# A fifth block problem with seven products in the FFN, its first two products in the opening, and the rest rows inside the output product

## The chip, the cores and the metric

The kernel runs on one core of one Trainium2 chip. TensorE (PE; its weight loads are PEld) multiplies, VectorE (DVE) and ScalarE (ACT) work on elements, GpSimd (POOL) does a few small operations and issues the DMAs that add to their destination, and SyncE (SP) issues the other DMAs. The metric is the device time of one launch in microseconds (us); lower is better. A measured number is the median of several executions. Durations and waits come from one further execution that the hardware profiler recorded.

## The reference

Two layers over 512 rows of width 1024: a gated mixer of three branches (retention, chunked attention, differential attention), then a SwiGLU FFN, each followed by a normalisation. The change touches the FFN and its normalisation:

```python
D_MODEL, SEQ, DEPTH, FFN_HIDDEN = 1024, 512, 2, 2816
...
        x = _layer_norm(DEEPNORM_ALPHA * x + mix, ln1_g[l], ln1_b[l])

        u = jnp.einsum('bsd,df->bsf', x, w_ffn_in[l])
        u_gate, u_up = jnp.split(u, 2, axis=-1)
        ffn = jnp.einsum('bsf,fd->bsd', jax.nn.silu(u_gate) * u_up, w_ffn_out[l])
        x = _layer_norm(DEEPNORM_ALPHA * x + ffn, ln2_g[l], ln2_b[l])
```

All numbers are float32. The FFN's inner width 2816 is 22 tiles of 128.

## The kernel before

**Arithmetic.** Each float32 operand is carried as a pair of float32r tiles, the rounded part (`hi`) and what is left (`lo`). `mm3` (line 124) multiplies two pairs by three matmuls: hi by hi, hi by lo, lo by hi. A weight block (128 partitions x 2048, 1 MiB) is loaded into a staging buffer (`st`, four of them), cast by ScalarE to `wh` and subtracted by VectorE to `wl` (lines 157 and 158 in `Wt`, 315 and 322 in `Staged`). There are three `wh`/`wl` pairs (`AHEAD`). `run_items` works through a list of items; before an item runs it fetches the blocks of later ones until three are ready or in work. An item's `groups` are functions called at the `between()` places inside it. The tool that builds the program then orders the instructions of each engine by its own model of costs, with the program's order as priority, unless `keep_in_program_order` or `issue_after` ties them.

**Plain items.** `u_ffn(i)` makes one inner tile: `proj_T` for the gate and for the up part, each 8 steps of `mm3` with 512 moving columns, so 48 matmuls; the result stands transposed (features in partitions). ScalarE's silu and VectorE's product follow in `ffn_done`.

**Block problems.** `u_fin(pb, kind)` makes four inner tiles (512 gate and 512 up columns) at once. The product of two matrices of 2 x 2 blocks is made with seven block products in place of eight (m1, m2, y, x, v, g, h in `u_two`). Each product is one block of weights and `product(acts, name, j, wt)` for j = 0, 1: 4 steps of `mm3`, so 24 matmuls of 512 columns. The left operands are combinations of quarters of the input, made by `Quarters.left` (y, x) and `Quarters.right` (v, g); m1, m2 and h use quarters as they are, m1 and m2 those of the first 256 rows. The right operands are sums of weight blocks: made by DMA (`more`, a second DMA issued on POOL that adds to the staged block) or by VectorE (lines 254, 260 and 283). The class of the problem says which: `Chain` keeps one buffer from m1 to h and adds to it three times; `Close` and `Early` load a sum `a` (for y), a sum `c` (for g), and add `d` and `e` on VectorE; `Early` loads the block for `e` a second time in x. Products x, g and h add onto the PSUM banks of m1, and v onto those of y, so two banks are held from m1 to h and two from y to v. The results stand with rows in partitions; `s_turn` transposes them on TensorE (line 1444) and ScalarE copies them from PSUM.

Before, four block problems p, q, r, u make inner tiles 0 to 15, and `u_ffn(16)` to `u_ffn(21)` the six others. In the opening of the FFN, while the normalisation of the first half still goes on, stand p's m1, p's m2, `u_ffn(16)`, `u_ffn(17)`, `u_ffn(18)`, then p's y. The split of `u_ffn(16)`'s block is made in two parts (`half_split`, `s_other_half`). `s_turned(1)` makes the second 256 rows of the transposed input `x1T` (`to_T`: line 588, then `xTh` by ScalarE and `xTl` by VectorE); `s_x1` and `s_x1r` call `left` and `right`; `s_natural` scales and shifts the rows and stores them.

**Output product.** `fout_items(0)` and `(1)` (o and w) multiply inner tiles 0-3, 4-7 and 8-11, 12-15, again with seven products each. Their left operands are `Twins`, made by `s_ready`, `s_differ`, `s_sums` and `s_rest`. Inner tiles 16 to 21 (from `REST` on) go by plain products in `fout_rest`: for each of four row tiles t and two column halves, 6 steps of `mm3`, 18 matmuls. These stand at the very end, in `front`, `middle` and `back`; `plus` adds each result to `z` (lines 1298, 1300), the last one takes statistics (line 531), and `normalise` or, in the last layer, `finish` (lines 537 to 545) closes a row tile. In the last layer the very last tile is made in two halves of 256 columns. In layer 0, `transposes(0)` and `transposes(1)` stand midway in two tiles, `to_T(0)` follows, and `opening[l + 1].early()` loads the first block of the next layer; two more tiles stand behind them.

Of the kernel before, what the change touches and what calls it, by code (L numbers as in the profile page):

```python
# [58 lines left out]
def trunk(ctx, tc, x_in, xT_in, w_in, ret_norm_g, da_norm_g, lq1, lk1, lq2, lk2, w_a, w_b, w_c, b_merge, w_out,  # L59
# [26 lines left out]
    def bank(name="ps"):  # L86
        return psp.tile([P, 512], F32, tag="ps", name=name)
# [36 lines left out]
    def mm3(ps, lh, ll, rh, rl, start, stop, onto=False):  # L124
        nc.tensor.matmul(ps, lh, rh, start=start, stop=False, skip_group_check=onto)  # L125
        nc.tensor.matmul(ps, lh, rl, start=False, stop=False, skip_group_check=onto)  # L126
        nc.tensor.matmul(ps, ll, rh, start=False, stop=stop, skip_group_check=onto)  # L127
# [282 lines left out]
    def proj_T(act, wt, c0, nk=KT, ps=None, half=None):  # L410
# [281 lines left out]
    def layer(l):  # L692
# [714 lines left out]
        def ffn_spec(i):  # L1407
            w = w_ffn_in[l]
            return ([w[:, P * i:P * i + P], w[:, FFN + P * i:FFN + P * i + P]], KT)
# [95 lines left out]
        def half_split(i):  # L1505
            def fn():
                half_split.wt = w = Wt(*ffn_spec(i), later=True)
                w.load(0, KT)
                w.split(0, KT // 2)
                return w  # L1510
            return fn

        def s_other_half():
            half_split.wt.split(KT // 2, KT)

        def u_ffn(i):
            def fn(wt):
                pg = proj_T(x1T, wt, 0)
                between()
                pu = proj_T(x1T, wt, P)  # L1520
                ffn_done(i, pg, pu)
            return [half_split(i) if i == 16 else ffn_spec(i)], fn

        def fout_items(gi):

            r0, kh = GROUPS[gi]
            hv = Chain(w_ffn_out[l], r0, kh)
            w = {}

            def it(name, *adds):  # L1530
                def fn(wt):
                    if name == "m1" and gi == 0:
                        load_res(x2, saved[2 * l])
                    on = {"x": "m1", "g": "m1", "h": "m1", "v": "y"}.get(name, name)
                    for j in range(2):
                        w[on, j] = product([hid[r0 + k] for k in range(kh)], name, j, wt, w.pop((on, j), None))
                        for i, hf, op in adds:
                            plus(x2, 2 * i + j, hf, w[on, j], op)
                        if name in ("m2", "v", "h"):
                            w.pop((on, j))  # L1540
# [6 lines left out]
        def fout_rest():  # L1547

            A, B = slice(0, 256), slice(256, 512)
            rk = FT - REST - 4  # L1550
            b1, b3 = (([w_ffn_out[l][P * REST:P * REST + P * 4, 512 * hf:512 * hf + 512]], 4) for hf in range(2))
            b2 = ([w_ffn_out[l][P * REST + P * 4:P * FT, :]], rk)
            W, ahead = {}, {}

            def tile(t, hf, midway=None):
                at = [(W[("b1", "b3")[hf]], k, 0) for k in range(4)]
                at += [(W["b2"], k, 512 * hf) for k in range(rk)]
                end = last and t == NT - 1
                for cols in (A, B) if end and hf else (slice(0, 512),):
                    n = cols.stop - cols.start  # L1560
                    ps = bank("pf")[:, :n]
                    for i, (w, k, c) in enumerate(at):
                        if i == len(at) // 2 and midway:
                            midway()
                        a, sl, cs = hid[REST + i], slice(P * t, P * t + P), slice(c + cols.start, c + cols.stop)
                        mm3(ps, a.hi[:, sl], a.lo[:, sl], w.hi[:, k, cs], w.lo[:, k, cs], i == 0, i == len(at) - 1)
                    plus(x2, t, hf, ps, ALU.add, True, cols, (A, B) if end and not hf else (cols,))
                if hf:
                    x2["n"].finish(t) if last else x2["n"].normalise(t)

            def front(*_):
                x2["n"] = Norm(x2["z"], v["g2"], v["b2"], bcast_rows(ln2_g[l:l + 1]),
                               bcast_rows(ln2_b[l:l + 1]), xTs[l + 1], out if last else saved[2 * l + 1], xfs[l + 1])
                tile(0, 0)
                between()
                tile(1, 0)

            def middle(*_):
                if last:
                    for t, hf in (0, 1), (1, 1), (2, 0), (2, 1), (3, 0), (3, 1):  # L1580
                        tile(t, hf)
                    return
                n = x2["n"]
                tile(0, 1)
                opening[l + 1].early()
                tile(1, 1)
                tile(2, 0, lambda: n.transposes(0))
                tile(3, 0, lambda: n.transposes(1))
                n.to_T(0)
                ahead[nc.scalar] = last_of(nc.scalar)  # L1590

            def back(*_):
                tile(2, 1)
                tile(3, 1)
                quarters(l + 1)
                ahead[nc.vector] = last_of(nc.vector)
                behind[opening_fn[l + 1]] = list(ahead.values())

            def block(name, spec):

                def fn():
                    W[name] = Wt(*spec)
                    return W[name]
                return fn

            def held(name):
                return lambda: W[name]

            parts = [([block("b1", b1), block("b2", b2)], front), ([block("b3", b3), held("b1"), held("b2")], middle)]
            return [(p,) for p in parts + ([] if last else [([held("b2"), held("b3")], back)])]  # L1610

        p, q, r, u = u_fin(0, ffn_opening), u_fin(1, Close), u_fin(2, Close), u_fin(3, Close)
        proj["next"] = p["m1"][1]
        o, w = fout_items(0), fout_items(1)
        for (specs, fn), *groups in [
            (([ffn_opening.m1_high], p["m1"][1]), [], [s_turned(1)]), (([ffn_opening.m2_high], p["m2"][1]), [s_other_half], [s_natural(0)]), (u_ffn(16), [s_x1(0)], [s_x1(1)]),
            (u_ffn(17), [s_x1(2)], [s_x1(3)]), (u_ffn(18), [s_natural(1)], [s_x1r(0), p["c"]]), (p["y"], [s_x1r(1)], [s_x1r(2)]),
            (u_ffn(19), [s_x1r(3)], [s_natural(2)]), (p["v"], [s_natural(3)], [q["a"]]), (p["x"],), (q["m1"],), (p["g"],), (q["y"], [s_turn(0, 0)]), (p["h"], [q["c"]]),
            (q["v"], [r["a"]]), (q["m2"], [s_turn(0, 1)]), (q["x"],), (r["m1"],), (q["g"],), (r["y"], [s_turn(1, 0)]), (q["h"], [r["c"]]),
            (r["v"], [u["a"]]), (r["m2"], [s_turn(1, 1)]), (r["x"],), (u["m1"],), (r["g"],), (u["y"], [s_turn(2, 0)]),  # L1620
            (r["h"], [u["c"]], [s_ready(0, 0)]), (u["v"], [s_ready(0, 1)]), (u["m2"], [s_turn(2, 1)]), (u["x"],),
            (o["m1"], [s_differ(0, 0)], [s_differ(0, 1)]), (u["g"],), (o["m2"], [s_sums(0, 0)], [o["c"]]), (u["h"], [s_turn(3, 0)]),
            (o["y"], [s_sums(0, 1)]), (u_ffn(20), [s_rest(0, 0)], [s_rest(0, 1)]), (o["v"], [s_turn(3, 1)]),
            (o["x"], [s_ready(1, 0)], [s_ready(1, 1)]),
            (w["m1"], [s_differ(1, 0)]), (o["g"], [s_differ(1, 1)], [w["c"]]), (w["m2"], [s_sums(1, 0)]), (o["h"], [s_sums(1, 1)]),
            (w["y"], [s_rest(1, 0)]), (u_ffn(21), [s_rest(1, 1)], [s_hid(16, 17, 18)]), (w["v"], [s_hid(19, 20, 21)]), (w["x"],),
            (w["g"],), (w["h"],), *fout_rest(),
        ]:
            item(specs, fn, *groups)

# [59 lines left out]
```

## Time and profile before

| what | us |
|---|---|
| median of 3 runs | 1856.95 (1856.66 to 1857.39) |
| the profiled execution | 1857.49, its span 1855.7 |
| layer 0: opening of the FFN (p's m1) | from 588.6 |
| layer 0: first output product (o's m1) | from 781.8 |
| layer 1: opening of the FFN (p's m1) | from 1511.6 |
| layer 1: `u_ffn(16)` | from 1525.1 |
| layer 1: first output product (o's m1) | from 1704.8 |
| layer 1: rest rows | from 1815.4 |

Times inside are counted from the span's start. In a row of a group, "x" is the count, then come busy time, the mean length of one in ns, and the engine's idle time before them with what ended it. Matmuls overlap on TensorE: the length of one record is longer than the step from one to the next. In the view of the chain a row has start, share of the chain's time, and what.

### The profile page before, as it was taken

How to read it: one execution, taken by the hardware profiler on the slowest of the kernel's cores; microseconds unless marked ns; L12 is line 12 of the kernel's file. 1: busy time of each engine (PE TensorE's matmuls, PEld its weight loads, DVE VectorE, ACT ScalarE, POOL GpSimd, SP SyncE). 2: the span in 40 equal slices, each digit the busy share in tenths (PEclk: the TensorE clock that was granted, in tenths of full speed). 3: DMA queues.
4: the chain of work that ended last, by engine and by line, in shares of the span. 5: the costliest groups of instructions: out<-in, count | busy, mean ns of one | idle time of the engine just before them, and what ended most of it. 6: DMA issues, size and time to landing. Idle time of an engine off the chain costs nothing. (4 is left out here: it accounts for less than half of the span.)

```text
span 1855.7 us, 23376 instructions
## 1 busy us (share of the span) xinstructions
PE 1846.6 (100%) x8788; PEld 1545.0 (83%) x8788; DVE 1354.0 (73%) x2080; ACT 1002.7 (54%) x1621; POOL 135.8 (7%) x152
## 2 busy tenths in 40 slices
PE   9999999999999999999999999999999999999998
PEld 8888888888887888888888888888888888888887
DVE  6766756777679666778697767567775896677886
ACT  5555555576546445554355556556765464455540
POOL 2001000000001100010010010000000011000100
PEclk9999999999999999999999999999999999999999
DMA  9685444332456777698376844533325577776871
GB/s 284 187 269 151 124 142 132 92 125 80 125 159 162 187 200 183 193 223 207 131 227 188 248 123 140 161 114 97 114 68 148 144 181 183 196 205 191 204 195 46
DMA packets 235456, 302.89 MB, mean 163 GB/s; under 512 B 8772, under 2 KB 127664, under 8 KB 235344
## 3 DMA queue, kind: packets, MB, share of 16 engines
q1 hardware_dynamic: 205888, 244.09, 40.5%
q0 software_dynamic: 29312, 57.06, 17.9%
q8 instruction: 69, 1.13, 0.2%
q14 instruction: 43, 0.35, 0.1%
q10 hardware_dynamic: 144, 0.26, 0.0%
HBM read 279.31 MB, written 22.07 MB: 162 GB/s over the span
## 5 line engine op out<-in xcount | busy, mean ns | idle before, releaser
L322 DVE TENSOR_TENSOR wl<-st,wh 128x2048 fp32r<-128x2048 f32 (+1 forms) x143 | 320.8, 2245 | 127.7 <-ACT wh L315 126.7
L125 PE MATMUL pt<-xTh,wh 128*128 128x512 f32 x960 | 377.2, 394 | 0.0
L127 PE MATMUL pt<-xTh,wl 128*128 128x512 f32 x960 | 374.2, 390 | 0.0
L126 PE MATMUL pt<-xTl,wh 128*128 128x512 f32 x960 | 374.0, 390 | 0.0
L315 ACT CAST wh<-st 128x2048 fp32r<-128x2048 f32 x140 | 267.8, 1913 | 184.2 <-PE pf L127 97.9
L158 DVE TENSOR_TENSOR wl<-st,wh 128x1024 fp32r<-128x1024 f32 (+2 forms) x186 | 199.9, 1095 | 57.1 <-ACT wh L157 44.0
L157 ACT CAST wh<-st 128x1024 fp32r<-128x1024 f32 (+2 forms) x186 | 172.1, 948 | 124.8 <-PE pt L126 60.5
L127 PEld LDWEIGHTS pt<-xTh,wl 128*128 128x128 f32 x960 | 180.3, 188 | 38.3
L125 PEld LDWEIGHTS pt<-xTh,wh 128*128 128x128 f32 x960 | 180.7, 188 | 36.1
L126 PEld LDWEIGHTS pt<-xTl,wh 128*128 128x128 f32 x960 | 180.5, 188 | 36.0
L125 PE MATMUL pf<-wh,xTh 128*128 128x512 f32 x336 | 132.3, 394 | 0.0
L127 PE MATMUL pf<-wh,xTl 128*128 128x512 f32 x336 | 131.7, 392 | 0.3 <-DVE xTl L115 0.2
L126 PE MATMUL pf<-wl,xTh 128*128 128x512 f32 x336 | 130.8, 389 | 0.0
L125 PE MATMUL pf<-wh,s12h 128*128 128x512 f32 x256 | 101.0, 395 | 0.0
L125 PE MATMUL pf<-wh,s43h 128*128 128x512 f32 x256 | 100.2, 391 | 0.0
L126 PE MATMUL pf<-wl,s12h 128*128 128x512 f32 x256 | 99.9, 390 | 0.0
L126 PE MATMUL pf<-wl,s43h 128*128 128x512 f32 x256 | 99.7, 389 | 0.0
L127 PE MATMUL pf<-wh,s43l 128*128 128x512 f32 x256 | 99.4, 389 | 0.0
L127 PE MATMUL pf<-wh,s12l 128*128 128x512 f32 x256 | 99.2, 390 | 0.0
L841 ACT COPY tc<-pf 128x512 f32<-128x512 f32 x84 | 48.7, 589 | 79.9 <-PE pf L127 77.1
L127 PEld LDWEIGHTS pf<-wh,xTl 128*128 128x128 f32 x336 | 63.1, 188 | 15.7 <-DVE xTl L115 2.5
L125 PEld LDWEIGHTS pf<-wh,xTh 128*128 128x128 f32 x336 | 63.1, 188 | 12.9 <-issue 0.4
(360 smaller groups left out, 3647.4 us busy)
## 6 DMA issues: line engine op xcount, KB each, us to landing
st<-in_w_in SPq DMA_DIRECT2D x53, 1024.0 KB, 5.4
st<-in_w_ffn_in SPq DMA_DIRECT2D x38, 1024.0 KB, 5.4
st<-in_w_in SPq DMA_DIRECT2D x48, 512.0 KB, 4.5
st<-in_w_ffn_out SPq DMA_DIRECT2D x22, 1024.0 KB, 7.7
st<-in_w_ffn_in POOLq DMA_DIRECT2D x20, 1024.0 KB, 10.4
st<-in_w_ffn_out POOLq DMA_DIRECT2D x16, 1024.0 KB, 8.8
st<-in_w_in POOLq DMA_DIRECT2D x12, 1024.0 KB, 11.7
st<-in_w_ffn_in SPq DMA_DIRECT2D x24, 512.0 KB, 5.3
```

The costliest lines, as they stand in the source:

```text
L125: nc.tensor.matmul(ps, lh, rh, start=start, stop=False, skip_group_check=onto)
L126: nc.tensor.matmul(ps, lh, rl, start=False, stop=False, skip_group_check=onto)
L127: nc.tensor.matmul(ps, ll, rh, start=False, stop=stop, skip_group_check=onto)
L157: return [nc.scalar.copy(self.hi[:, a:b], self.st[:, a:b]), nc.vector.tensor_sub(self.lo[:, a:b], self.st[:, a:b], f(self.hi[:, a:b]))]
L158: nc.vector.tensor_sub(self.lo[:, a:b], self.st[:, a:b], f(self.hi[:, a:b]))]
L315: nc.scalar.copy(self.hi, st)
L322: nc.vector.tensor_sub(self.lo[:, k], self.st[:, k], f(self.hi[:, k]))
L841: nc.scalar.copy(t[to, j], ps)
```

## The change

Inner tiles 16 to 19 become a fifth block problem, `t = u_fin(4, Early)`, with `pb` 4; `u_ffn(20)` and `u_ffn(21)` remain and move to the opening. `t["m1"]` and `t["m2"]` stand right after p's, where `u_ffn(16)` and `u_ffn(17)` stood; t's other products are interleaved with p's and q's. `half_split` and `s_other_half` go. `s_turn_rest` transposes t's rows, two inner tiles a call, in q's m2 and x. The rest rows are now two items, one for each half of the columns: `u_rest(0)` between o's y and v, `u_rest(1)` between w's x and g. Each loads its block of tiles 16-19 and the block of tiles 20 and 21, so the latter is loaded and split twice. The statistics and the closing of a row tile therefore come from `u_rest(1)` for tiles 0 and 1 and from w's products for tiles 2 and 3; in the last layer the last product's second part (j = 1) is made in two halves of columns. `s_shift` loads the scale and shift rows in w's v.

```diff
-    def product(acts, name, j, wt, ps=None):
+    def product(acts, name, j, wt, ps=None, cols=slice(0, 512)):
...
-            mm3(ps, hi[:, sl], lo[:, sl], wt.hi[:, k], wt.lo[:, k], k == 0 and not onto, k == wt.nk - 1, onto)
+            mm3(ps[:, cols], hi[:, sl], lo[:, sl], wt.hi[:, k, cols], wt.lo[:, k, cols], k == 0 and not onto,
+                k == wt.nk - 1, onto)
...
-            return [half_split(i) if i == 16 else ffn_spec(i)], fn
+            return [ffn_spec(i)], fn
+
+        A, B = slice(0, 256), slice(256, 512)
+
+        def closed(t):
+            x2["n"].finish(t) if last else x2["n"].normalise(t)
...
+                    final = gi == len(GROUPS) - 1 and name in ("m2", "g", "h")
                     for j in range(2):
+                        end = last and final and name != "m2" and j
+                        ps = w.pop((on, j), None)
+                        for cols in (A, B) if end and name == "h" else (slice(0, 512),):
+                            ps = product([hid[r0 + k] for k in range(kh)], name, j, wt, ps, cols)
+                            for i, hf, op in adds:
+                                plus(x2, 2 * i + j, hf, ps[:, cols], op, final, cols,
+                                     (A, B) if end and name == "g" else (cols,))
+                        if name not in ("m2", "v", "h"):
+                            w[on, j] = ps
+                        if final and name == "h":
+                            closed(2 + j)
+                        between()
+                    if final and name == "h" and not last:
+                        quarters(l + 1)
+                        ahead[nc.vector] = last_of(nc.vector)
+                        behind[opening_fn[l + 1]] = list(ahead.values())
...
+        def s_turned2():
+            n = x2["n"]
+            n.transposes(1)
+            n.to_T(0)
+            ahead[nc.scalar] = last_of(nc.scalar)
...
+        def u_rest(hf):
+
             rk = FT - REST - 4
+            c0 = 512 * hf
+            blocks = [([w_ffn_out[l][P * REST:P * REST + P * 4, c0:c0 + 512]], 4),
+                      ([w_ffn_out[l][P * REST + P * 4:P * FT, :]], rk)]
...
+                plus(x2, t, hf, ps, ALU.add, hf and t < 2)
+                if hf and t < 2:
+                    closed(t)
+
+            def fn(b1, b2):
                 n = x2["n"]
+                for t in range(NT):
+                    tile(t, b1, b2, (lambda: n.transposes(0)) if hf and t == 3 and not last else None)
+                    if hf and t == 0 and not last:
+                        opening[l + 1].early()
+                    between()
+            return blocks, fn
+
+        def s_turn_rest(fp):
+            def fn():
+                for f in (fp, fp + 1):
+                    ps = bank("ph")
+                    for t in range(NT):
+                        nc.tensor.transpose(ps[:, P * t:P * t + P], nat[4, t][:, P * f:P * f + P], ident)
+                    t = hid[REST + f] = g(name="fth")
+                    nc.scalar.copy(t, ps)
+            return fn
...
-            (([ffn_opening.m1_high], p["m1"][1]), [], [s_turned(1)]), (([ffn_opening.m2_high], p["m2"][1]), [s_other_half], [s_natural(0)]), (u_ffn(16), [s_x1(0)], [s_x1(1)]),
-            (u_ffn(17), [s_x1(2)], [s_x1(3)]), (u_ffn(18), [s_natural(1)], [s_x1r(0), p["c"]]), (p["y"], [s_x1r(1)], [s_x1r(2)]),
...
+            (([ffn_opening.m1_high], p["m1"][1]), [], [s_turned(1)]), (([ffn_opening.m2_high], p["m2"][1]),),
+            (t["m1"], [], [s_x1(0)]), (t["m2"], [s_x1(1)], [s_x1(2)]), (u_ffn(20), [s_x1(3)], [s_x1r(0), p["c"]]),
+            (p["y"], [s_x1r(1)], [s_x1r(2)]), (u_ffn(21), [s_x1r(3), t["a"]], [s_natural(0)]),
+            (p["v"], [s_natural(1)]), (p["x"], [s_natural(2)]), (t["y"], [s_natural(3)]), (p["g"],), (t["v"], [s_turn(0, 0)]), (p["h"], [t["c"]], [q["a"]]),
+            (t["x"], [s_turn(0, 1)]), (q["m1"],), (t["g"],), (q["y"],), (t["h"], [q["c"]]),
+            (q["v"], [r["a"]]), (q["m2"], [s_turn_rest(0)]), (q["x"], [s_turn_rest(2)]), (r["m1"],), (q["g"],), (r["y"], [s_turn(1, 0)]), (q["h"], [r["c"]]),
...
+            (o["y"], [s_sums(0, 1)], [s_hid(20, 21)]), (u_rest(0), [s_rest(0, 0)], [s_turn(3, 1)], [s_rest(0, 1)], [s_ready(1, 0)]), (o["v"],),
...
+            (w["y"], [s_rest(1, 0)]), (w["v"], [s_rest(1, 1)], [s_shift]), (w["x"],), (u_rest(1),),
+            (w["g"], tail), (w["h"],),
```

`tail` is `[s_turned2]` in layer 0 and empty in the last layer.

More of the change, by code (lines that the diff above doesn't have):

```diff
@@ L1503, in u_fin @@
                          functools.partial(gate_half, pb), functools.partial(gated, pb))
[L1505 to L1514, printed above, removed]
         def u_ffn(i):
@@ L1533, in fn @@
                         load_res(x2, saved[2 * l])
+                        x2["n"] = Norm(x2["z"], v["g2"], v["b2"], None, None, xTs[l + 1],
+                                       out if last else saved[2 * l + 1], xfs[l + 1])
                     on = {"x": "m1", "g": "m1", "h": "m1", "v": "y"}.get(name, name)
+                    final = gi == len(GROUPS) - 1 and name in ("m2", "g", "h")
                     for j in range(2):
[L1536 to L1540, printed above, removed]
+                        end = last and final and name != "m2" and j
[14 more added lines that the diff above has]
+                        behind[opening_fn[l + 1]] = list(ahead.values())
                 return [getattr(hv, name)], fn
@@ L1545, in fout_items @@
                     "m2": it("m2", (0, 0, add)), "v": it("v", (0, 1, add)), "g": it("g", (1, 1, sub)), "h": it("h", (1, 0, add))}
-        def fout_rest():
-            A, B = slice(0, 256), slice(256, 512)
-            rk = FT - REST - 4
[L1551 to L1582, printed above, removed]
-                n = x2["n"]
[L1584 to L1610, printed above, removed]
@@ new lines, in s_turn_rest @@
+        def s_turn_rest(fp):
[7 more added lines that the diff above has]
+            return fn
+        p, t, q, r, u = u_fin(0, ffn_opening), u_fin(4, Early), u_fin(1, Close), u_fin(2, Close), u_fin(3, Close)
@@ L1613, in layer @@
         proj["next"] = p["m1"][1]
         o, w = fout_items(0), fout_items(1)
+        tail = [] if last else [s_turned2]
         for (specs, fn), *groups in [
-            (([ffn_opening.m1_high], p["m1"][1]), [], [s_turned(1)]), (([ffn_opening.m2_high], p["m2"][1]), [s_other_half], [s_natural(0)]), (u_ffn(16), [s_x1(0)], [s_x1(1)]),
-            (u_ffn(17), [s_x1(2)], [s_x1(3)]), (u_ffn(18), [s_natural(1)], [s_x1r(0), p["c"]]), (p["y"], [s_x1r(1)], [s_x1r(2)]),
-            (u_ffn(19), [s_x1r(3)], [s_natural(2)]), (p["v"], [s_natural(3)], [q["a"]]), (p["x"],), (q["m1"],), (p["g"],), (q["y"], [s_turn(0, 0)]), (p["h"], [q["c"]]),
@@ L1623, in layer @@
-            (o["y"], [s_sums(0, 1)]), (u_ffn(20), [s_rest(0, 0)], [s_rest(0, 1)]), (o["v"], [s_turn(3, 1)]),
-            (o["x"], [s_ready(1, 0)], [s_ready(1, 1)]),
+            (r["h"], [u["c"]], [s_ready(0, 0)]), (u["v"],), (u["m2"], [s_turn(2, 1)], [s_ready(0, 1)]), (u["x"],),
+            (o["m1"], [s_differ(0, 0)], [s_differ(0, 1)]), (u["g"],), (o["m2"], [s_sums(0, 0)], [o["c"]]), (u["h"], [s_turn(3, 0), s_hid(16, 17)], [s_hid(18, 19)]),
+            (o["y"], [s_sums(0, 1)], [s_hid(20, 21)]), (u_rest(0), [s_rest(0, 0)], [s_turn(3, 1)], [s_rest(0, 1)], [s_ready(1, 0)]), (o["v"],),
```

18 lines of the change are left out of this document (12 added, 6 removed).

## The prediction

> **What bounds it.** I read the page first, then who waited for whom on TensorE, then the chain of waits in the middle of layer 1's FFN.
>
> ```profile
> span 1855.7 us, 23376 instructions
> PE 1846.6 (100%) x8788; PEld 1545.0 (83%) x8788; DVE 1354.0 (73%) x2080; ACT 1002.7 (54%) x1621; POOL 135.8 (7%) x152
> PEclk9999999999999999999999999999999999999999
> ```
>
> ```profile
> PE warm L645 <- POOL ident masks.py:199: 1.5, 1, 1.5
> PE pf L127 <- DVE xTl L115: 0.2, 1, 0.2
> ```
>
> TensorE is busy for 1846.6 of 1855.7 us at the full granted clock, and the second view says that in the whole run it sat idle for others 1.7 us, 1.5 of them before its first instruction. So the time is the number of TensorE instructions by their step, plus a head and a tail. The busy time hides the step, since matmuls overlap; the chain shows it:
>
> ```profile
> 1591.93 0.23 PE pf L125
> ...
> 1598.51 0.23 PE pf L127
> 1598.74 0.87 PE ph L1444 x8
> 1599.62 0.23 PE pf L125
> ...
> 1602.38 0.23 PE pf L125
> ```
>
> From 1591.93 to 1598.51 stand 29 matmuls of 512 columns: 6.58 / 29 = 0.227 us each. Eight transposes of `s_turn` put 1599.62 - 1598.51 - 0.227 = 0.88 us between two matmuls, and the 12 matmuls after them take 2.76 in place of 2.72: 0.92 a group.
>
> **TensorE's count.** Per layer, four `u_ffn` items of 48 matmuls go (192) and seven products of 2 x 4 x 3 = 24 come (168). All have 512 moving columns. 24 fewer by 0.227 is 5.4 us a layer, **-10.9** for two. `s_turn_rest` adds 16 transposes a layer in two groups of eight: 4 x 0.92 = **+3.7**. The rest rows keep their number (8 tiles of 18) wherever they stand. In the last layer the narrow matmuls at the end fall from 36 to 24; their step is in the chain at the end:
>
> ```profile
> 1846.06 0.12 PE pf L126
> ...
> 1848.34 0.13 PE pf L127
> 1848.49 0.43 DVE z L1300
> 1848.95 0.44 DVE bn L531
> ...
> 1851.10 0.74 DVE z L544
> 1851.85 0.66 DVEq L1686
> ```
>
> 36 x 0.12 - 18 x 0.227 = 0.24 extra before, 24 x 0.12 - 12 x 0.227 = 0.16 after: -0.1. TensorE's sum is **-7.3 us**, if nothing new makes it wait.
>
> On the transposes the Trainium skill speaks against the change: "TensorE: Matmul & The Clock Gate", Part 4 (PE-mode transpose), gives about 275 ns for one transpose in a kernel. By that 32 of them would cost 8.8 us and not 3.7, an estimate from that page.
>
> ```profile
> L1444 PE MATMUL ph<-ident,fth 128*128 128x128 f32 x64 | 8.3, 273 | 0.0
> ```
>
> The row has 273 ns as the length of a record, but 64 of them cover 8.3 us, 0.13 each, and the chain has 0.11: they overlap as matmuls do. I keep 3.7.
>
> **The tail.** Before, output tile 2 is finished while tile 3 still has 18 wide and 36 narrow matmuls to go (4.1 + 4.3 us). After, `closed(2)` follows the first half of `w["h"]`, and only 24 narrow ones (2.9 us) follow. VectorE's rows:
>
> ```profile
> 1841.87 1.40 DVE L542 SCALAR_TENSOR_TENSOR z<-z,mv,bc 128x512 f32<-128x512 f32 x2
> 1843.19 1.41 DVE L544 SCALAR_TENSOR_TENSOR z<-z,rs,bc 128x512 f32<-128x512 f32 x2
> 1844.52 0.68 DVE L1300 TENSOR_TENSOR z<-z,pf 128x512 f32<-128x512 f32 x1
> 1846.34 0.42 DVE L1300 TENSOR_TENSOR z<-z,pf 128x256 f32<-128x256 f32 x1 [0.35 <-PE pf L127]
> ```
>
> Tile 2 needs add and statistics (0.7 each), the two small steps (0.3), L542 and L544 (1.3 each as they follow one another): 4.3 us from about 0.3 us after its last matmul. Tile 3's first half adds 0.9 (0.46 + 0.46). VectorE is free for the last half at 0.3 + 4.3 + 0.9 = 5.5 us, where that half is ready at 2.9 + 0.3 = 3.2. So the end moves 2.3 us later. If tile 2's last pair is put behind tile 3's, it still has to be done before the end: not under 1.1. I take **+2.2**.
>
> **The opening.** VectorE and ScalarE are nearly full where the first two products of the new problem now stand:
>
> ```profile
> 1511.00:1525.00 14.00, 13.84 (x68) 10.79 (x67) 13.29 (x26) 11.62 (x25) 1.21 (x3) 1.00 0.72 150
> 1525.00:1536.00 11.00, 11.00 (x50) 9.10 (x49) 10.19 (x19) 8.99 (x16) 0.66 (x1) 1.00 0.88 257
> 1743.00:1783.00 40.00, 40.00 (x182) 33.18 (x181) 35.70 (x41) 20.99 (x22) 3.85 (x3) 1.00 0.88 205
> ```
>
> The columns after the window are PE, PEld, DVE, ACT, POOL, clock, DMA share, GB/s. In the first, 52 matmuls and 16 transposes need 13.5 of 14 us, so half a microsecond per layer is lost here already. New demands: `t.m1` needs its whole `wl` when `u_ffn(16)` needed a half, and `t.m2` is cast on ScalarE in one piece where `u_ffn(17)` was cast in two:
>
> ```profile
> 1517.43 1.05 ACT L157 CAST wh<-st 128x1024 fp32r<-128x1024 f32 x1 [1.55 <-PE pf L127]
> 1518.38 1.01 ACT L588 ACTIVATE xf<-px,colv 128x256 f32<-128x256 f32 x2
> ```
>
> ```profile
> 1519.30 1.22 DVE L158 TENSOR_TENSOR wl<-st,wh 128x1024 fp32r<-128x1024 f32 x1
> 1520.43 0.75 DVE L115 TENSOR_TENSOR xTl<-xf,xTh 128x256 fp32r<-128x256 f32 x2
> ```
>
> ```profile
> L322 DVE TENSOR_TENSOR wl<-st,wh 128x2048 fp32r<-128x2048 f32 x137 | 313.6, 2290 | 127.7 <-ACT wh L315 126.7
> L315 ACT CAST wh<-st 128x2048 fp32r<-128x2048 f32 x140 | 267.8, 1913 | 184.2 <-PE pf L127 97.9
> ```
>
> Queued behind that cast on ScalarE are the last casts of `x1T`; behind the subtraction on VectorE are their low parts, and `p.m2` waits for those. 1.91 in place of 1.05 and 2.29 in place of 1.22 make them 0.9 to 1.1 us later. Against that, `s_natural(0)` and its store leave this stretch, both new products need only the first 256 rows, and `u_ffn(20)`, the first that needs all rows, starts 2 x 24 x 0.227 = 10.9 us later than `u_ffn(16)` did, near 1536 in place of 1525. TensorE's order here is mixed between the two halves of a product, so late parts can be stepped around. Bounds: -0.5 a layer (what is lost now goes) to +2 (both delays in full). I take +0.25, **+0.5** for both.
>
> **The rest of VectorE.** Per layer the new problem has 7 splits of 2.29 for 4 of 2.44, two block sums of 2.29, six results of 0.68, and the rest rows load their last two rows' block twice (2.44): +17 us on an engine 73% busy; ScalarE gets as many casts (1.91 each) and six copies, about 13 us at 54%. It lies beside TensorE while each `wl`, made two items ahead, is ready in time. The tightest stretch is the second output group, 35.7 of 40 us in the last window above, which keeps its load but loses `u_ffn(21)`, its pause. Two waits are new. An item of rest rows holds two of the three `wh`/`wl` buffers to its end, so the cast for the item after next (`o["x"]`, and `w["h"]`) waits on ScalarE until the rest rows' last reads; behind it wait casts of the twins in the first case, of `xT` in the second. From 1 us before the end of the rest rows to the next item's end there are 6.6 us; cast and subtraction take 4.2. I cost this at nothing, with 2 us in hand; a miss is up to 2 us a layer. At the layer boundary the second set of transposes comes 36 matmuls (8.2 us) before the first product that reads them, where it came 45 (10.2) before. ScalarE needs 4 x 1.01 us for the eight L588 by the row above, and no more than that again for the casts; the first product reads four of the eight, the next one the others 5.4 us later. Nothing. The moved loads (`s_shift`'s four rows, `early`'s block) go out on SP 27 us or more before their use.
>
> **Sum:** -7.3 + 2.2 + 0.5 = -4.6 us on the profiled execution's 1857.5 us (span 1855.7), 0.25%. The median shown, 1856.95, is 0.5 lower: **1852.4**.
>
> **Rivals.** *Late sums of blocks (slower).* Products y and g take a block that one DMA loads and a second, on POOL, adds to.
>
> ```profile
> q1 hardware_dynamic: 205888, 244.09, 40.5%
> q0 software_dynamic: 29312, 57.06, 17.9%
> ...
> st<-in_w_ffn_in SPq DMA_DIRECT2D x38, 1024.0 KB, 5.4
> st<-in_w_ffn_in POOLq DMA_DIRECT2D x20, 1024.0 KB, 10.4
> ```
>
> ```profile
> DMA to landing us min/median/max: 8.4/9.8/15.4
> ```
>
> The last column of the issues is the median from issue to landing, and the last row is for every adding DMA of line 181. The queues' rows are MB and shares of the 16 engines' span: 3.2 us for 1 MiB loaded, 6.1 for 1 MiB added. The change adds three loads and two sums a layer, 22 us, mostly in the 113 us from `p.m1` to `q.v`; I count about 100 us of transfers there, 0.89, a share that the last window bears. But with four staging buffers, two problems at once hold `p`'s two, `t`'s two. By the order of items, `t`'s block for y gives its buffer back after the sum for `t.v`, and `q.a` gets one only near 1591.5, when `t.x` has used `d` (`p["g"]` ends at 1585 and frees the `wh` buffer; cast 1.9, split 2.3, sum 2.3). Load 5.4, sum 10.4, cast and split 4.2: ready at 1611.5, for `q["y"]` at 1613.8. With the longest landing (15.4) and a load of 10 it is 7 us late; at 2.3 late in each layer the gain is gone. Behind the waiting cast on ScalarE stand the next casts and the copies out of PSUM. For it: 2 us of room is the least of all steps. Against it: before, the last window ran at a DMA share of 0.88 without one wait of TensorE. At 6 us in each layer the time is 1852.4 + 12 = **1864**; chance 0.12. At about 2 a layer it is **1856.5**, no change; 0.15. The Trainium skill, "DMA: Bandwidth & Descriptors" (Anatomy of one DMA - SWDGE (gpsimd) path), gives 2.0 us + bytes / 436e3, an estimated 4.4 us for 1 MiB: by it nothing would be late, but the row's 9.8 decides.
>
> *A jammed opening.* The last casts of `x1T` stop `p.m2` for 2 us a layer: -7.3 + 2.2 + 4 = -1.1, **1855.8**; 0.13. For it: the second view's one wait in the middle is this one.
>
> *Transposes at their full record.* 32 x 0.273 = 8.7 for 3.7: +0.4, **1857.4**; 0.03, since the chain speaks against it. That the page named above gives the same length is told there.
>
> **Chances.** Forecast 0.57, with 1850.4 to 1854.4 as its own range (the tail at 1.1 and no stall in the openings below, 2 us more above). A measurement tells 0.2%, 3.7 us, from no change, so the edge is 1853.2; I put four fifths of the forecast below it. Faster 0.46, same 0.42 (the rest of the forecast, 0.15, 0.13, 0.03), slower 0.12. The range goes up to 1857.6, over the small delays and the transposes, and leaves out late blocks in full.
>
> **What would show it.** TensorE with 8 instructions fewer in layer 0 (-24 + 16) and 14 fewer in layer 1 (6 fewer by the narrow ones); -7 us between the first matmul and the last; the tail from the last matmul to the end about 2 us longer, with L542 and L544 without a gap; no new releaser of TensorE in the view of waits but `xTl`. Wrong, if that view names casts or splits (`wh`, `wl`) in the items `t` and `q`, or ScalarE waits for a DMA there and TensorE behind it.

## The result, and the profile after

| | us |
|---|---|
| before, median of 4 runs | 1856.94 (1856.66 to 1857.39) |
| after, median of 4 runs | 1887.91 (1887.20 to 1890.22) |
| ratio after to before | 1.0169, 95% interval 1.0151 to 1.0186 |
| the profiled execution of after | 1887.43, its span 1885.7 |

The change makes the kernel 31 us slower. The forecast was 1852.4 with a range up to 1857.6; it was wrong, and in the sign.

The first rows of the page of after:

```profile
span 1885.7 us, 23407 instructions
PE 1851.4 (98%) x8766; PEld 1543.7 (82%) x8766; DVE 1384.3 (73%) x2100; ACT 1024.9 (54%) x1643; POOL 140.7 (7%) x156
```

TensorE has 8766 instructions where it had 8788, as forecast, and yet the span grew by 30.0 us. The view of waits, for TensorE (total us, times, longest):

```profile
PE pf L125 <- DVE z L1301: 13.3, 3, 6.4
PE pf L125 <- DVE tc L852: 5.5, 2, 3.1
PE pf L127 <- DVE hidl L115: 3.2, 4, 1.7
PE pf L126 <- DVE wl L322: 1.7, 2, 1.2
PE warm L646 <- POOL ident masks.py:199: 1.5, 1, 1.5
```

Before, this view held 1.7 us; now it has 25.2. Waits are not the whole loss: matmuls after a long wait are slower. So I added up, over all pairs of matmuls that follow one another, the time from start to start less the usual step (0.227 us at 512 columns). That excess was 9.3 us before and is 45.4 after, 36.1 more. With the saved instructions (-7.3) and a tail that grew from 7.24 to 8.59 us (last matmul's end to the span's end) this makes +30.1, the 30.0 of the spans. By place, both layers together, in us:

| place | after | what TensorE waits for |
|---|---|---|
| w's y to w's v | 17.6 | `plus` of w's y (z L1301) |
| t's g | 9.3 | the subtraction in t's x (tc L852) |
| first rest item | 5.0 | low parts of inner tiles 16 to 21 (hidl) |
| r's m1 | 2.4 | low part of its block (wl) |

These four places hold 34 of the 36.1 us.

**The largest place.** The chain of waits in layer 1 (start us, length, what):

```profile
1817.79 13.04 DMA st<-in_w_ffn_out
...
1830.93 1.91 ACT wh L315
...
1832.86 0.56 DVE wl L322
...
1835.07 0.69 DVE z L1301
...
1835.89 0.77 PE pf L125
1836.66 0.43 PE pf L126
```

`w` is a `Chain`: one buffer carries the blocks of m1, y, x and h, and the sum for x may only start when y's block is split, at 1817.5. It lands at 1830.83, and ScalarE's cast waits for it, then VectorE's low part. The first matmul of w's v follows at 1835.89. But v does not use this sum; x does. What v needs is the PSUM bank of y, which `plus` of y must have read. Why that read is late, the timeline of VectorE shows (start, length, line, [idle before it <- what ended the wait]):

```profile
1824.69 0.68 DVE L115 TENSOR_TENSOR qgl<-hf,qgh 128x512 fp32r<-128x512 f32 x1
1832.86 2.29 DVE L322 TENSOR_TENSOR wl<-st,wh 128x2048 fp32r<-128x2048 f32 x1 [7.48 <-ACT wh L315]
1835.07 0.68 DVE L1301 TENSOR_TENSOR z<-z,pf 128x512 f32<-128x512 f32 x1
```

The low part of x's block, made two items ahead, stands in VectorE's order in front of `plus` of y. The low part waits for a DMA; everything behind it waits too; TensorE waits for what is behind.

Before, `u_ffn(21)` stood between y and v. The sum for w's x was issued at 1771.66 and landed 8.5 us later (the second fence is the answer for that one DMA); ScalarE's cast at 1783.03 waited for a buffer that TensorE freed, not for the DMA:

```profile
1771.66 1.28 POOL L181 DMA_DIRECT2D st<-in_w_ffn_out  x1 [8.79 <-DVE wl L322]
```

```profile
DMA to landing us min/median/max: 8.5/8.5/8.5
```

```profile
1783.03 1.92 ACT L315 CAST wh<-st 128x2048 fp32r<-128x2048 f32 x1 [2.29 <-PE pf L127]
```

**The clock.** In the windows of after (busy time of PE, PEld, DVE, ACT, POOL; granted clock, DMA share, GB/s) the clock falls with the wait and comes back late:

```profile
1829.00:1836.00 7.00, 0.60 (x4) 0.20 (x2) 3.14 (x3) 4.31 (x4) 0.56 (x1) 0.79 0.65 247
1836.00:1842.00 6.00, 6.00 (x19) 4.74 (x20) 3.90 (x5) 0.00 (x0) 0.72 (x1) 0.67 0.82 134
```

The steps behind the wait are 0.43 us (last row of the chain above), w's v takes 7.95 and 7.45 us in the two layers in place of 5.44, and 4.5 of the 17.6 us are this. The Trainium skill, "TensorE: Matmul & The Clock Gate", Part 1 (the HAM clock gate), says that the clock is halved after an idle window of about 3.4 us; the 6.6 us wait and steps of 0.43 in place of 0.227 agree.

**The second place** is of the same kind, in the chain of layer 1:

```profile
1601.44 6.38 DMA st<-in_w_ffn_in
...
1608.38 13.36 DMA st<-in_w_ffn_in
...
1621.82 1.92 ACT wh L315
...
1623.76 2.29 DVE wl L322
1626.06 0.61 DVE tc L852
```

This is `t["c"]`, the sum for t's g: load, adding DMA, cast, low part. Behind that low part stands the subtraction of t's x, which reads the banks onto which t's g accumulates. VectorE is idle for 9.85 us before that low part, so it is not short of time here. The load could not start before a staging buffer came free at 1601.4.

### The profile page after: what moved, and what is told of

It reads as the page before. It is cut to its first block, busy times and chain, and to the rows that moved or that the text cites. A ratio compares the mean times of both kernels' runs of the same rounds, so it can differ in the third digit from the quotient of the medians.

```text
span 1885.7 us, 23407 instructions
## 1 busy us (share of the span) xinstructions
PE 1851.4 (98%) x8766; PEld 1543.7 (82%) x8766; DVE 1384.3 (73%) x2100; ACT 1024.9 (54%) x1643; POOL 140.7 (7%) x156
## 4 chain that ended last, share of the span: by engine, by line
PE 85%; DMA 6%; DVE 5%; ACT 2%; issue 2%; POOL 0%; DVEq 0%; ACTq 0%; POOLq 0%; SPq 0%
PE pt L125 13%; PE pt L127 13%; PE pt L126 13%; PE pf L125 12%; PE pf L127 12%; PE pf L126 12%; DMA st<-in_w_ffn_in 4%; DVE wl L322 2%; DMA st<-in_w_ffn_out 2%; ACT wh L315 2%; PE ptr L503 1%; PE psc L464 1%; PE pco L1073 1%; PE psc L463 1%; PE pdo L1150 1%
## 5 line engine op out<-in xcount | busy, mean ns | idle before, releaser
L322 DVE TENSOR_TENSOR wl<-st,wh 128x2048 fp32r<-128x2048 f32 (+1 forms) x159 | 352.8, 2221 | 143.0 <-ACT wh L315 142.1
L315 ACT CAST wh<-st 128x2048 fp32r<-128x2048 f32 x154 | 294.3, 1913 | 249.4 <-PE pf L127 136.8
L125 PE MATMUL pt<-xTh,wh 128*128 128x512 f32 x832 | 327.6, 394 | 0.0
L127 PE MATMUL pt<-xTh,wl 128*128 128x512 f32 x832 | 324.5, 390 | 0.0
L126 PE MATMUL pt<-xTl,wh 128*128 128x512 f32 x832 | 324.3, 390 | 0.0
L127 PEld LDWEIGHTS pt<-xTh,wl 128*128 128x128 f32 x832 | 156.3, 188 | 33.1
L125 PEld LDWEIGHTS pt<-xTh,wh 128*128 128x128 f32 x832 | 156.7, 188 | 31.0
L126 PEld LDWEIGHTS pt<-xTl,wh 128*128 128x128 f32 x832 | 156.5, 188 | 31.1
L125 PE MATMUL pf<-wh,xTh 128*128 128x512 f32 x384 | 151.3, 395 | 0.2
L126 PEld LDWEIGHTS pf<-wl,xTh 128*128 128x128 f32 x384 | 72.2, 188 | 16.8 <-DVE wl L322 2.5
## 6 DMA issues: line engine op xcount, KB each, us to landing
st<-in_w_ffn_in POOLq DMA_DIRECT2D x24, 1024.0 KB, 10.9
```

The costliest lines, as they stand in the source:

```text
L315: nc.scalar.copy(self.hi, st)
L322: nc.vector.tensor_sub(self.lo[:, k], self.st[:, k], f(self.hi[:, k]))
```

## The experiments

Theory A, held through all of them: the change takes away work that stood between the start of a late sum and its use, and the instructions that wait for the sum stand, in the orders of ScalarE and VectorE, in front of reads of PSUM that TensorE needs sooner. Theory B: VectorE and ScalarE simply have too much to do in these stretches. Other rivals stand with the runs. Each kernel is the changed one (1887.9) with the edit shown. Times are medians of 4 runs, where no other number is given.

### The sum for w's x made another way

```diff
+    class Near(Chain):
+        def y(self):
+            return self.block(self.a)
+        def v(self):
+            d = self.load(1, 1)
+            b = self.block(d)
+            nc.vector.tensor_add(self.a, self.a, d)
+            return b
...
-            hv = Chain(w_ffn_out[l], r0, kh)
+            hv = (Near if gi else Chain)(w_ffn_out[l], r0, kh)
```

> Only the chain of the second output group is altered: the sum for w's x is no longer made by the adding DMA issued after w's y is split (it landed 13.0 us later) but by VectorE from the block that w's v loads anyway, one addition of 2.3 us a layer. Theory A (the late sum, and the reads of PSUM that stand behind its split in VectorE's order, stop TensorE between w's y and v; 13.2 us of wait and 4.4 us of slow steps in the two layers): 1887.9 - 17.6 = 1870, at least 13 us gained, and the waits of TensorE for z L1301 nearly gone. Theory B (VectorE as a whole is full in this stretch, and any work there makes it later): 2 x 2.3 us slower, 1892.

Measured: 1869.78 us, -18.1; ratio to before 1.0066 (1.0051 to 1.0081). The view of waits has one 0.5 us left for `plus`, at the very end:

```profile
PE pf L125 <- DVE z L1301: 0.5, 1, 0.5
```

Theory A's number. VectorE got work added (2 x 2.3 us) and the kernel was faster: theory B falls for this place.

### The sum for t's g by VectorE

```diff
+    class Fifth(Early):
+        def x(self):
+            b = self.block(self.d)
+            self.e, self.c = self.load(1, 0), self.load(0, 1)
+            nc.vector.tensor_add(self.e, self.e, self.d)
+            nc.vector.tensor_add(self.c, self.c, self.__dict__.pop("d"))
+            return b
...
-(p["h"], [t["c"]], [q["a"]])
+(p["h"], [], [q["a"]])
```

`d` already holds more than the second block here, so the operand of t's g has other values; the work is the same.

> Only the fifth block problem is altered: its sum for product g is made by VectorE from a plain load and the block already loaded for x (one addition of 2.3 us a layer), in place of the adding DMA that landed 13.4 us after its issue. Theory A: the waits at t's g (5.9 us) and the slow steps behind them (3.4 us) go, 1887.9 - 9.3 = 1878.6; what stalls at r's m1 (2.5 us) may go too, since one transfer of 1 MiB and one adding of 1 MiB less stand in the queues: 1876. Theory B: VectorE has no room for 2.3 us more in this stretch, 1890 to 1892.

Measured: 1892.82 us (1889.46 to 1893.86). Neither number of theory A, and near theory B's. The waits say why: tc L852 is gone from TensorE's list, and these have come.

```profile
PE pf L126 <- DVE wl L322: 7.3, 4, 1.8
PE pf L125 <- ACT wh L315: 3.0, 4, 1.1
```

The timeline of ScalarE shows the place:

```profile
1628.68 1.91 ACT L315 CAST wh<-st 128x2048 fp32r<-128x2048 f32 x1 [11.45 <-DMA st<-in_w_ffn_in]
```

This is the block of q's y, whose sum (`q["a"]`) lands at 1628.6. VectorE is idle for 9.86 us before that block's low part, not overfull, so this is not theory B's mechanism. But the edit has a part in it: the load for this sum waits for the staging buffer that `d` holds, and goes out when the second addition is done, at 1611.49, where in after it went out behind the one addition at 1608.89. In after that cast started at 1627.85, behind its DMA too, but the wait at t's g had pushed q's y back and hid it. The wait moved one item on (2.9 and 2.8 us of excess there), and the excess at r's m1 rose to about 5 us in each layer (1.6 and 0.8 in after); what makes that one late was not followed. Two sums in a row are late; a mend has to bring both forward, and the loads of both start when a staging buffer comes free.

### The splits of inner tiles 16 to 21 earlier

```diff
-(u["x"],)
+(u["x"], [s_hid(16, 17)])
-(u["g"],)
+(u["g"], [s_hid(18, 19)])
-[s_turn(3, 0), s_hid(16, 17)], [s_hid(18, 19)])
+[s_turn(3, 0)], [s_hid(20, 21)])
-[s_sums(0, 1)], [s_hid(20, 21)])
+[s_sums(0, 1)])
```

> Only the places of the six splits of the inner tiles 16 to 21 are altered: two, two and one item earlier, ahead of the casts of the first rest item's blocks in ScalarE's order. Theory A (the low parts are late only because their high parts stand behind a cast that waits for the block's load): the first rest item loses its waits of 5.0 us in the two layers, 1882.9. Rival: the blocks of the rest item are late themselves, and TensorE waits for them in place of the low parts: at most 1 us gained, 1887.

Measured: 1888.40 us (1884.57 to 1890.48): no change. In its view of waits:

```profile
PE pf L125 <- DVE z L1301: 17.2, 5, 8.5
...
PE pf L127 <- DVE hidl L115: 0.5, 2, 0.3
```

The waits for low parts went from 3.2 to 0.5 us, the excess at the first rest item from 5.0 to 2.4. What was gained there was lost at w's v, where the excess rose from 17.6 to 20.8 us, and at r's m1 of layer 0 (1.6 to 5.3). The wait at w's v is set by a sum; that TensorE arrives earlier only makes it longer. Why r's m1, which lies ahead of the edit, got worse in this execution stays open.

### The order on VectorE and ScalarE, with the sum as late as before

The first kernel moved the low part of w's x alone behind the products of w's v, j = 0:

```diff
+        def x_high(self):
+            self.third = Staged(self.a, self.kh, later=True)
+            return self.third
+        def x_low(self):
+            self.third.low()
+            self.more(self.a, 1, 0)
...
-(w["v"], [s_rest(1, 1)], [s_shift])
+(w["v"], [s_rest(1, 1), w["low"]], [s_shift])
```

> Only the order on VectorE is altered: the low part of w's x, which waits for the late sum, is made behind the reads of PSUM of w's y and not ahead of them. The sum comes as late as before. Theory A (VectorE's order): TensorE does w's v (5.4 us) during the wait and stops only ahead of w's x, by about 1 us in each layer, without slow steps: 1887.9 - 2 x 5.6 - 4.4 = 1872. Rival (the late sum alone sets the end, wherever its split stands): the stall moves to w's x with the same length, 1888.

Measured: 1889.29 us (1887.19 to 1891.61), and TensorE still waits ahead of w's v. The timelines of ScalarE and of VectorE:

```profile
1832.54 1.90 ACT L315 CAST wh<-st 128x2048 fp32r<-128x2048 f32 x1 [11.12 <-DMA st<-in_w_ffn_out]
1834.34 0.61 ACT L109 CAST qhh<-hf 128x512 fp32r<-128x512 f32 x1
```

```profile
1834.99 0.69 DVE L115 TENSOR_TENSOR qhl<-hf,qhh 128x512 fp32r<-128x512 f32 x1 [9.31 <-ACT qhh L109]
1835.60 0.68 DVE L1301 TENSOR_TENSOR z<-z,pf 128x512 f32<-128x512 f32 x1
```

The low part no longer stands ahead of `plus`, but the cast that waits for the same sum stands on ScalarE ahead of `qhh`; `qhl` on VectorE waits for `qhh`, and `plus` is behind `qhl`. There are two queues, not one. The next kernel gave the cast and the low part a later place in the program: `x_room` hands out an empty block and `x_fill` makes it in a group after all of w's y (the diff below without its `issue_after` and with `s_rest(1, 1)` left in w's v).

> The cast on ScalarE and the low part on VectorE of w's x, which both wait for the late sum, are made behind all of w's y; in the run with the low part alone moved, a high part of another operand (qhh) stood behind the waiting cast on ScalarE, its low part on VectorE waited for it, and the read of PSUM behind that. The sum comes as late as before. Theory A, with both queues: TensorE does w's v during the wait and stops ahead of w's x, by 1 to 2 us in a layer (landing, then cast and low part, 4.2 us), with few slow steps: 1887.9 - 2 x 5 - 4 = 1874. Rival (the late sum alone sets the end): 1888.

Measured: 1889.55 us (1887.75 to 1891.83). The builder set the cast ahead of `qhh` and the low part ahead of `plus` again, so the run has after's order and settles nothing. A third kernel ties the order, and makes `s_rest(1, 1)` an item earlier:

```diff
+        def x_room(self):
+            self.room = types.SimpleNamespace()
+            return self.room
+        def x_fill(self):
+            with tc.issue_after(last_of(nc.vector)), tc.issue_after(last_of(nc.scalar)):
+                vars(self.room).update(vars(self.x()))
...
-(w["y"], [s_rest(1, 0)]), (w["v"], [s_rest(1, 1)], [s_shift])
+(w["y"], [s_rest(1, 0), s_rest(1, 1)], [w["fill"]]), (w["v"], [s_shift])
```

> As the run before it meant to: the cast and the low part of w's x now really stand behind the high and low part of the last operand (qhh, qhl) and behind both reads of PSUM of w's y, on ScalarE and on VectorE; in that run they had stayed ahead of qhh, and its time says nothing on the question. The sum comes as late as before. Theory A (the two queues): TensorE runs w's v while the sum lands, and waits 0.3 to 2 us ahead of w's x, so about 6 us of wait and 2 us of slow steps go in each layer: 1872. Rival (the late sum sets the end, wherever the instructions that wait for it stand): 1888.

Measured: 1873.11 us (1872.15 to 1873.57), -14.8; ratio to before 1.0087 (1.0073 to 1.0100). VectorE's timeline, and the landing of the sum for w's x that was issued at 1811.48:

```profile
1818.96 0.68 DVE L115 TENSOR_TENSOR qhl<-hf,qhh 128x512 fp32r<-128x512 f32 x1
1820.47 0.69 DVE L1301 TENSOR_TENSOR z<-z,pf 128x512 f32<-128x512 f32 x1 [0.83 <-PE pf L127]
1823.19 0.69 DVE L1301 TENSOR_TENSOR z<-z,pf 128x512 f32<-128x512 f32 x1 [2.03 <-PE pf L127]
1826.64 2.29 DVE L322 TENSOR_TENSOR wl<-st,wh 128x2048 fp32r<-128x2048 f32 x1 [2.77 <-ACT wh L315]
```

```profile
DMA to landing us min/median/max: 13.1/13.1/13.1
```

The sum is as late as in after (13.1 us against 13.0), and nearly the whole loss at this place is gone: both reads of PSUM now wait only for TensorE, w's v runs while the sum lands, and only w's x loses time: 0.5 us in layer 1 (5.91 us in place of 5.44) and 1.6 in layer 0 (7.01), where the sum took 14.3 us. So the late sum alone cost 2.0 us; its place in two queues made that 17.6. The Trainium skill, "Perfetto Trace Analysis" (Per-engine timelines, Tensor Engine Instruction), says that VectorE, ScalarE and GpSimd are strictly first in, first out; the rows of these runs agree.

### Distance, with the order as it was

```diff
-(w["m2"], [s_sums(1, 0)]), (o["h"], [s_sums(1, 1)]),
-(w["y"], [s_rest(1, 0)]), (w["v"], ...
+(w["m2"], [s_sums(1, 0)], [s_sums(1, 1)]),
+(w["y"], [s_rest(1, 0)]), (o["h"],), (w["v"], ...
```

> Half of the pause that the changed kernel took out of the second output group is given back with work that is there anyway: o's h (5.4 us of TensorE) stands between w's y and v, not ahead of y. Theory A (the distance from y to x is shorter than the sum takes): the wait shrinks from 6.6 to about 1.2 us and most slow steps go, 7 us in each layer: 1873. Rival (the stretch holds more work of VectorE and ScalarE than fits, whatever the order): 1888.

Measured: 1869.59 us (1869.09 to 1869.98), -18.3; ratio 1.0069 (1.0054 to 1.0084). One item of 5.4 us in the gap left by `u_ffn(21)` takes away the whole loss, more than the 14 us expected: no wait at w's v is left.

### The wait filled with transposes

```diff
+        def s_warm():
+            ps = bank("ph")
+            for k in range(56):
+                nc.tensor.transpose(ps[:, P * (k % 4):P * (k % 4) + P], ident, ident)
...
-(w["y"], [s_rest(1, 0)])
+(w["y"], [s_rest(1, 0)], [s_warm])
```

> 56 transposes of the identity (0.11 us each, 6.1 us) stand between w's y and v in both layers, in the 6.6 us in which TensorE waits there; nothing else is altered, and the sum comes as late as before. Theory (the wait itself and the lower granted clock after it are two costs): the wait shrinks to about 0.5 us with no change of the end, the steps after it keep 0.227 us, and 2 x 2 us are gained: 1884. Rival (the slow steps after the wait come from something else, a busy memory or late low parts): 1888 as before, with the same slow steps.

Measured: 1888.14 us (1886.64 to 1893.47): the rival's time, but not its slow steps. The windows of the transposes and of w's v:

```profile
1830.00:1838.40 8.40, 6.63 (x59) 6.25 (x57) 3.00 (x3) 4.31 (x4) 0.41 (x1) 1.00 0.60 218
1838.40:1844.00 5.60, 5.56 (x25) 4.62 (x25) 3.96 (x5) 0.00 (x0) 0.88 (x1) 1.00 0.72 121
```

The clock stays at 1.00, and w's v takes 5.56 us in both layers in place of 7.95 and 7.45. So the slow steps do come from TensorE's idle time. They were not won as time, since in this execution the sum took 14.3 and 14.6 us to land in place of 13.1 and 13.0, and t's g lost 2 us more in layer 1; the first is measured, whether the edit caused it is open.

### The stretch of t and q, and all together

```diff
+    class Kept(Close):
+        def m1(self):
+            self.a = self.load(0, 0)
+            b = self.block(self.a)
+            self.more(self.a, 0, 1)
+            return b
...
-u_fin(1, Close)
+u_fin(1, Kept)
-(t["v"], [s_turn(0, 0)]), (p["h"], [t["c"]], [q["a"]])
+(t["v"], [s_turn(0, 0), t["c"]]), (p["h"],)
```

> In the stretch of t and q: the load for t's g is asked for ahead of that of q's m1 (one item earlier), so it takes the staging buffer that comes free 2.8 us sooner; and q's y takes the buffer that q's m1 has used, to which the second block is added, so one load of 1 MiB a layer and the buffer for it are saved. Theory (the two sums are late because four staging buffers and two adding DMAs at once pace them): the waits at t's g (5.9 us) go and none comes at q's y, 1887.9 - 9.3 = 1878.6. Rival (as in the run with the sum by VectorE, the lateness only moves on, here to q's y, where the sum now starts only after q's m1 is split): within 2 us of 1888.

Measured: 1878.07 us (1876.89 to 1881.04), -9.8; ratio 1.0118 (1.0101 to 1.0135). The waits for tc L852 are gone and none has come at q's y. With `Near` as well:

> The sum of w's x by VectorE (alone 1869.8) and the two edits in the stretch of t and q together. If both places are independent, the gains add: 1869.8 - 9.3 = 1860.5. If the second only moves its wait on, 1869.

Measured: 1859.71 us, median of 10 (1858.09 to 1862.45); ratio 1.0016 (1.0007 to 1.0026). The two places are independent. Then `Kept` for q, r and u, without `r["a"]` and `u["a"]`:

> As the combined run (1859.7), and r and u too take y's block from the buffer that their m1 has used, so two more loads of 1 MiB a layer go and r's m1 is asked for about 9 us earlier. Theory (the load of r's m1 stands behind another load and two adding DMAs, 10.8 us from issue to landing, 3.9 us of waits in the two layers): 1855.7. Rival (the adding DMA, now issued only after m1's split, is late for r's or u's y): 1860 or more.

Measured: 1855.89 us, median of 11 (1854.88 to 1858.37); ratio 0.9998 (0.9989 to 1.0007). No wait is left at r's m1. Last, with the splits of the inner tiles earlier:

> As c6, with the six splits of inner tiles 16 to 21 earlier as well. Alone that took the waits for low parts in the first rest item from 5.0 to 2.4 us, but the time stayed (the waits at w's v grew); with that place mended by the other sum: 1.5 us below c6, 1854. Rival (the splits only crowd out others): at or above c6.

Measured: 1854.99 us, median of 11 (1853.83 to 1858.37); ratio to before 0.9990 (0.9982 to 0.9999). The page, and the one row of TensorE's waits beside its first instruction's:

```profile
span 1853.2 us, 23387 instructions
...
PE 1840.4 (99%) x8766; PEld 1538.8 (83%) x8766; DVE 1388.2 (75%) x2102; ACT 1024.9 (55%) x1643; POOL 138.3 (7%) x154
```

```profile
PE pf L125 <- DVE z L1301: 2.4, 3, 1.2
```

This is the fastest version, by a tenth of a per cent, at the edge of what can be told apart. All of the change's own work is in it, and VectorE is fuller than in after (75% for 73%); beside the new places of sums and splits, the sums kept in one buffer save three loads of 1 MiB a layer, and one adding DMA a layer has become an addition on VectorE. The excess over the usual step is 13.0 us, where before had 9.3 and after 45.4.

## Why the prediction was wrong

**TensorE's count, -7.3: right.** 22 instructions fewer, as counted. In the last kernel TensorE's time from the first matmul to the last is 3.8 us below that of before: -7.3 with 3.7 of excess more (9.3 to 13.0), so the count is seen once the waits are gone.

**The tail, +2.2: right in its mechanism, a little large.** It measured +1.35 (7.24 to 8.59 us). TensorE also waits 0.5 us in front of the last half's matmuls for the add of the half before; that stands in the excess above, and with it the end is 1.85 us later. VectorE does run tile 2's closing without a gap into the add of the last half, as forecast; the timeline of VectorE in after:

```profile
1877.07 1.41 DVE L545 SCALAR_TENSOR_TENSOR z<-z,rs,bc 128x512 f32<-128x512 f32 x2
1878.39 0.41 DVE L1301 TENSOR_TENSOR z<-z,pf 128x256 f32<-128x256 f32 x1
```

**The opening, +0.5: right.** In the window of after that answers to the one of before TensorE is busy for 13.87 of 14 us, where it was 13.84. By the steps it loses 1.15 us there, where it lost 0.93: 0.2 us a layer, for 0.25 forecast.

```profile
1526.40:1540.40 14.00, 13.87 (x67) 10.65 (x66) 13.32 (x24) 11.64 (x22) 1.21 (x3) 1.00 0.82 174
```

**"The rest of VectorE", costed at nothing: this step failed.** The working said: "It lies beside TensorE while each `wl`, made two items ahead, is ready in time." It also named the place: the second output group "keeps its load but loses `u_ffn(21)`, its pause". The pause was the point. I took it as rest for VectorE and looked at busy time: 35.7 of 40 us, so it fits. What `u_ffn(21)` gave was 10.9 us of distance between y, whose split starts the sum, and x, which needs it. The 40 us window of before (1743 to 1783), quoted against late sums since it had a DMA share of 0.88 and no wait, lies between the two pauses: TensorE is in `u_ffn(20)` until 1743.8 and in `u_ffn(21)` from 1782.8. It holds no y with its v and x right behind it, and could not bear that argument. Without `u_ffn(21)` the sum (13.0 us, with a DMA share of 1.12 from 1821 to 1829, where it had taken 8.5) with cast and low part (4.2) does not fit, and two in-order queues pass the wait on to a product that doesn't need the sum. Cost: 17.6 us, and 9.3 more at t's g by the same step: a low part that is not ready in time, with reads of PSUM behind it.

**The late sums of blocks, chance 0.12 and 0.15: the right rival, with a wrong place and price.** I followed one sum, `q["a"]`, and found 2 us of room. They were not there: its load, put at 1591.5, went out at 1608.89 in after, which is 1593.5 when the 15.4 us are taken off by which layer 1's opening stands later there, and the sum took 12.4 us in place of 10.4. Its neighbour `t["c"]`, loaded just ahead and used one item sooner, had less, and came first; the run with t's sum by VectorE then found `q["a"]` late as well, as that rival had it. I did not follow the `Chain` of w at all, though it is the same mechanism. And the price of a wait was taken as the lateness of the data alone: the casts and copies behind the waiting cast are named there, but neither they nor the reads of PSUM behind the low part nor the slow clock after the wait were in it. The sign given for being wrong did come: in the items of t ScalarE waits 8.6 us for a DMA, and TensorE behind it.

**The two new waits for `wh`/`wl` buffers, at most 2 us a layer:** not seen as such; the 5.0 us at the first rest item come from low parts whose high parts stand on ScalarE behind a cast that waits for its load, as the run with earlier splits showed.

The range left out the late blocks in full; that was a choice, and the profile had what was needed to see it: every sum's start, its landing and the item that uses it.

## What to carry to other kernels

Before an item is taken out from between two others, list each transfer that is started by the first and used by the second, and compare the new distance with its longest landing, not with the share of busy time. Then ask what stands behind the instruction that would wait, in every in-order queue that it passes through: a late block costs little where only its own product waits, and here 14.8 us less came from reordering alone. Making a sum on an engine that is 73% busy was cheaper than a DMA that is "free".

## What was not expected of the hardware

- A wait of 2.6 us was enough to lower the clock: at t's g in layer 1 TensorE waits from 1624.2 to 1626.8, and after seven steps of 0.22 to 0.39 us eight of about 0.43 us follow. The wait is shorter than the 3.4 us quoted above; here the measurement decides. The windows show it:

```profile
1624.00:1627.50 3.50, 1.06 (x5) 0.64 (x4) 3.47 (x4) 0.70 (x2) 0.00 (x0) 1.00 1.14 193
1627.50:1632.00 4.50, 4.50 (x15) 3.52 (x14) 3.39 (x3) 4.15 (x4) 0.00 (x0) 0.62 0.65 223
```

- Transposes alone kept the clock up: 56 of them, 0.11 us each and then a wait of up to 2 us, in the 8.4 us window above, and the granted clock stayed 1.00.
- The same adding DMA of 1 MiB took 8.5 us before and 13.0 after, 14.6 in another run, a spread larger than the room that was left. In after another adding DMA, issued at 1813.69, was under way until 1823.90; before, the one ahead of it had landed 0.4 us before it was issued. Whether that is the reason was not tested.
